# Two expert layers on one core: experts in groups of four with 32 places each, in place of pairs with 64

## The chip, the cores and the metric

One core of a Trainium2 chip runs the whole program once. The metric is the device time of that core in microseconds; lower is better. The program is a two-block network on 256 tokens of width 1024, in float32.

## The reference

The first block has two layers. Each is a mixer (a recurrence beside pooling in layer 0, attention beside a state-space model in layer 1) and then an expert layer. A second block of two layers follows. The change concerns the expert layers. Cut to what matters:

```python
def hier_moe(h, w_group, b_group, w_expert, b_expert, w_gate, w_up, w_down):
    '''Top-1 expert group, then top-2 experts in that group'''
    # 4 groups of 8 experts: each of 256 tokens goes to 2 of 32 experts
...
def routed_experts(hf, expert_idx, gates, w_gate, w_up, w_down):
...
    def run_block(args):
        tok, e, gt = args
        xb = h_pad[tok]
        hidden = jax.nn.silu(xb @ w_gate[e]) * (xb @ w_up[e])
        return (hidden @ w_down[e]) * gt[:, None].astype(xb.dtype)
```

`w_gate` and `w_up` of one expert are 1024 x 512, `w_down` is 512 x 1024, all float32: 6.29 MB an expert, 201.3 MB a layer. 512 places of tokens are spread over 32 experts, 16 on average. Evaluating the reference's routing on the given inputs, the fullest expert gets 26 tokens in layer 0 and 22 in layer 1.

## The kernel before

The order of the program is: recurrent mixer, expert layer 0, attention mixer, expert layer 1, second block. A scheduler orders each engine's instructions ahead of the run; on the chip each engine works through its list in order and waits on semaphores.

`moe` routes the tokens and then loops over 16 pairs of experts. `expert_pair` does, for a pair (64 places of an expert side by side make 128):

- **one-hot and gather** (L745, L757): VectorE makes a token-by-place matrix of zeros and ones. 32 products of 128 x 128 on TensorE pick the tokens out of the normed x (two float32r parts), giving `xe`, features on partitions, places along the free axis;
- **gate and up** (`both`, L763): for each of 8 blocks of features and each of the two experts one product with a stationary operand of 64 columns (that expert's places) and 512 moving columns of its weights. The two experts' results go to the two halves of the PSUM partitions. A float32 product is two MATMUL records;
- **hidden** (L784 to L790): silu on ScalarE, the product on VectorE, four transposes, a copy to SBUF (`hid`);
- **down** (L798): the same kind of products with `w_down`, by two halves of 512 output columns; ScalarE and VectorE scale by the gate and split in two parts (`y_hi` L801, `y_lo` L802);
- **scatter** (L808, L809, then L434): 8 products of 128 x 512 put the rows back to their tokens, VectorE adds to `x`.

`expert_weights` issues the loads of a pair on SyncE's queue (SP): 24 tiles of 512 KB (`wx`, 4 KB on each of 128 partitions), 8 of each matrix. A gate or up tile reads 4 KB in one piece for each partition, a down tile (`slab`, L734) two pieces of 2 KB. The tiles come by turns from three pools (`ring`, sizes `RINGS`): 17 tiles of the pool `u4`, 6 of the raw weights' pool `w`, 6 of the split weights' pool `hl`, 29 in all. In layer 0 from pair 4 on the ring is 6 + 6 + 6 = 18, because the next mixer's preparation (`middle`, that is `odd_prep` with `s5_prep`) takes `u4` tiles. A load waits until the products that read its place's last tile are done. The loads of the first pair are issued in `moe_ahead`, while the mixer still runs.

Before pair 4 stands a check, `overflowing`: each engine loads the largest count of an expert and branches. If it is over `SLOTS`, a loop over all experts follows for the tokens that found no place. With 64 places it is not taken on the given inputs.

The preparation of the attention mixer, a generator of small steps, runs between pairs 4 and 15 of layer 0, one or two steps a pair; its loads go through ScalarE's queue. In layer 1, `middle` is one small step.

Of the kernel before, what the change touches and what calls it, by code (L numbers as in the profile page):

```python
# [10 lines left out]
F32 = mybir.dt.float32  # L11
# [20 lines left out]
# where the odd mixer's projections and s5 steps stand in its attention  # L32
# [5 lines left out]
# where the even mixer's projections stand among its chunks  # L38
# [6 lines left out]
MAGIC = 1.5 * 2.0 ** 23  # added and taken off again, it rounds to an integer  # L45


def _parts(x):
    """x as a sum of three numbers of few bits"""
    out = []  # L50
    for bits in (10, 12, 24):
        e = math.floor(math.log2(abs(x)))
        step = 2.0 ** (e - bits + 1)
        v = math.floor(x / step) * step
        out.append(v)
        x -= v
    return out
# [29 lines left out]
class Stream:  # L87
    """Projections in the order in which they are added, by steps: the weights of a step are loaded
    and split ahead of its products."""
# [14 lines left out]
    def half(self):  # L104
        """half the products of a step"""
        self.products()
        self.then()
# [17 lines left out]
    def prepare(self):  # L125
        """the weights of the next steps"""
# [7 lines left out]
    def fetch(self, n=None):  # L134
        """the loads of all steps, or the first n, not their splits"""
# [3 lines left out]
    def through(self, n):  # L139
        """all steps of the first n items"""  # L140
# [4 lines left out]
class Model:  # L145
    def __init__(self, ctx, tc, I, out, taps=None):
# [13 lines left out]
        self.nsplit, self.on_pool = 0, 0     # of the weights' splits, every how many are gpsimd's  # L160
# [18 lines left out]
    def packed(self, name, parts):  # L179
        """a stage's constants, in one tile"""  # L180
# [12 lines left out]
    def u4(self, shape, dt=F32):  # L193
        """up to 4 KB a partition of longer-lived data"""
        return self.act.tile(list(shape), dt, tag="u4", name=self.name("u4"), bufs=23)

    def blocks(self, n, dt=F32):
        """n blocks [128, 256], as a list"""
# [51 lines left out]
    def rsqrt(self, out, src, scale, eps, shape):  # L250
        """out = (src * scale + eps) ** -0.5"""
# [25 lines left out]
    def split(self, hi, lo, src):  # L277
        """src (float32, SBUF) as hi + lo."""
# [16 lines left out]
    def proj_t(self, *a, **k):  # L295
        """ncol columns of h @ w, transposed: evac(block, psum [128, 256])."""
# [3 lines left out]
    def proj_t_steps(self, w, col0, xT, evac, ncol=512, pin=False):  # L300
        """proj_t, by its steps"""
# [15 lines left out]
    def item_t(self, w, col0, x, evac, ncol=512, pin=True, first=False):  # L317
        """proj_t for a stream; x() is the operand"""
# [24 lines left out]
    def item_n(self, w, col0, x, evac, row0=0, nk=None, pin=True):  # L343
        """512 columns of h @ w for a stream, tokens on partitions, over nk blocks of rows"""
# [21 lines left out]
    def proj_n(self, *a, **k):  # L366
        """ncol columns of h @ w, tokens on partitions: evac(token tile, psum [128, ncol])."""
# [32 lines left out]
    def rstd(self, t, eps=1e-6):  # L400
        """1 / rms of the rows of x's tile t, of which the mean squares are there"""
# [6 lines left out]
    def norm_t(self, gain, warm=0):  # L408
        """the normed x, transposed, as two float32r parts [128, 8, 256]."""
# [31 lines left out]
    def tick(self, first=1):  # L441
        """the next part of what x's new quarters, but the latest, give the router"""
# [7 lines left out]
    def out_proj(self, w, parts):  # L450
        """x += y @ w, y in parts: (first block of 128 features, hi, lo [128, 4, 256])"""
# [15 lines left out]
    def quarters(self, feeder):  # L467
        """x is there"""
# [6 lines left out]
    def begin(self):  # L475
        """before a stage's first step, if the one before leaves half of x's columns to be done between its steps"""
# [28 lines left out]
    def scales(self):  # L505
        """the tokens' scales: on partitions, and along the rows [128, 256]"""
# [8 lines left out]
    # -- mixture of experts -----------------------------------------------------  # L515
    def moe_ahead(self, l):
        """what an expert layer loads before its input is there"""
# [16 lines left out]
        return br, rings, self.expert_weights(l, 0, rings[0])  # L534
# [19 lines left out]
    def moe(self, l, ahead=None, middle=None, after=None):  # L554
# [10 lines left out]
        # normed x, tokens on partitions, as two parts (feature p * 8 + j at [j, p])  # L565
# [14 lines left out]
        def top(v, n):  # L580
            """the largest of [128, 2, n], and where it is first, as 0 and 1"""
# [18 lines left out]
        # by how many the experts of a group are outdone: those before count where equal  # L600
# [17 lines left out]
        # a token's place among those of an expert, from 1 on  # L618
# [8 lines left out]
        # the gates  # L627
# [42 lines left out]
        for pair in range(16):  # L670
            if pair == 4:
                self.keep_warm(WARM["check"])
                self.overflowing(l, over["n"], h_hi, h_lo, over["gates"])
            for _ in range((pair >= 4) + (pair in range(5, 12))):
                next(middle or iter(()), None)
            if pair == 15:
# [3 lines left out]
            if pair:  # L680
                weights = self.expert_weights(l, pair, rings[l == 0 and bool(middle) and pair >= 4], pair == 15 and after and after[1])
            self.rest = self.expert_pair(pair, weights, h_hi, h_lo, pos, gate, () if pair else (lambda: low(4), gates, beyond), pair == 15)
# [3 lines left out]
    def ring(self, *parts):  # L686
        """weight tiles of 4 KB, by turns out of the three pools"""
        tags = [t for t, m in enumerate(parts) for _ in range(m)]
        pools = ((self.act, "u4", 23), (self.wraw, "w", None), (self.wsp, "hl", None))
# [23 lines left out]
    def expert_weights(self, l, pair, tiles, between=None):  # L713
        """a pair of experts' weights"""
        nc, I = self.nc, self.I
        ee = (2 * pair, 2 * pair + 1)
# [1713 lines left out]
```

## Time and profile before

| what | value |
|---|---|
| median of 3 runs | 2854.08 us (2853.61 to 2862.12) |
| profiled execution, its span (the only time shown of it) | 2857.6 us |
| TensorE busy | 2676.7 us, 94% of the span |
| VectorE, ScalarE, GpSimd busy | 48%, 35%, 17% |
| loaded from HBM | 657.24 MB |
| expert layer 0, first gate product to last down product | 205.6 to 757.8 us |
| expert layer 1, the same | 950.9 to 1470.7 us |

A busy share of TensorE counts the time in which any product is under way. The profile gives, for each stretch, the share of full clock that was granted to TensorE (1.00 is 2.4 GHz) and the GB/s that the DMA engines moved. SPq rows are SyncE's issues of transfers; a row's second number is the time from the first to the last issue of the row.

### The profile page before, as it was taken

The page shows a single profiled execution, that of the slowest core. Times are in us where ns is not written, and L with a number is a line of the kernel's source. Part 1 is how long each engine was busy: PE and PEld are TensorE (multiplying, and loading weights), DVE is VectorE, ACT ScalarE, POOL GpSimd, SP SyncE. Part 2 cuts the span into 40 slices and gives each one's busy share as a digit, 9 for nine tenths or more (in the row PEclk, how much of TensorE's full clock was granted, in tenths as well). Part 3 has the DMA queues.
Part 4 walks back from the last instruction along what each step waited for, and adds up shares of the span by engine and source line. Part 5 has one row for each costly group of instructions (what it writes and reads, how often), then busy time and mean ns, then how long its engine had stood idle before and what let it go on. Part 6 is the DMA issues. An engine that isn't in the chain of part 4 may idle for free.

```text
span 2857.6 us, 43839 instructions
## 1 busy us (share of the span) xinstructions
PE 2676.7 (94%) x17593; PEld 2002.8 (70%) x17593; DVE 1359.5 (48%) x2263; ACT 1011.2 (35%) x1664; POOL 499.3 (17%) x428
## 2 busy tenths in 40 slices
PE   9989898889998999999999999999999999899998
PEld 8864344343577444443358998899988899899997
DVE  5641123231464321211146667746656576865664
ACT  6421121111235111111134546545444455554543
POOL 1110000010040000000022306511103132641110
PEclk9989899989999999999999999999999999999999
DMA  5359799989625889999945454355665555345564
GB/s 184 111 202 382 258 345 366 401 313 388 241 70 180 320 337 399 400 402 399 390 146 177 140 178 126 112 176 172 184 188 168 155 159 159 118 128 182 177 185 140
DMA packets 294463, 661.26 MB, mean 231 GB/s; under 512 B 36298, under 2 KB 42988, under 8 KB 294252
## 3 DMA queue, kind: packets, MB, share of 16 engines
q1 hardware_dynamic: 287796, 657.29, 66.5%
q8 instruction: 142, 2.33, 0.3%
q10 hardware_dynamic: 6456, 1.08, 0.3%
q14 instruction: 69, 0.57, 0.1%
HBM read 657.24 MB, written 1.05 MB: 230 GB/s over the span
## 4 chain that ended last, share of the span: by engine, by line
PE 50%; DVE 5%; POOL 3%; ACT 2%; issue 1%; DMA 1%; POOLq 0%; ACTq 0%; DVEq 0%; SPq 0%
PE ps_mm L291 36%; PE ps_mm L763 5%; PE ps_sml L798 3%; DVE whl L273 2%; PE ps_sml L757 1%; ACT whl L268 1%; DVE latri L2028 1%; POOL whl L273 1%; POOL xn L1979 1%; PE ps_sml L809 0%; PE ps_sml L1958 0%; POOL yf L1930 0%; DMA wx<-in_moe_w_gate_dram 0%; PE ps_sml L2078 0%; DMA wx<-in_moe_w_down_dram 0%
## 5 line engine op out<-in xcount | busy, mean ns | idle before, releaser
L291 PE MATMUL ps_mm<-u,whl 128*128 128x256 f32 x8448 | 1055.1, 286 | 27.5 <-POOL whl L273 17.4
L291 PEld LDWEIGHTS ps_mm<-u,whl 128*128 128x128 f32 x8448 | 1031.9, 193 | 40.8 <-POOL whl L273 19.4
L273 DVE TENSOR_TENSOR whl<-w,whl 128x1024 fp32r<-128x1024 f32 x432 | 557.7, 1295 | 418.4 <-ACT whl L268 411.6
L268 ACT ACTIVATE whl<-w 128x1024 fp32r<-128x1024 f32 x472 | 496.6, 1057 | 503.3 <-PE ps_mm L291 436.4
L763 PE MATMUL ps_mm<-wx,xe 128*64 128x512 f32 x2048 | 465.7, 607 | 0.0
L291 PE MATMUL ps_mm<-whl,u 128*128 128x512 f32 x1440 | 345.3, 396 | 6.1 <-ACT whl L268 3.2
L763 PEld LDWEIGHTS ps_mm<-wx,xe 128*64 128x64 f32 x2048 | 144.9, 139 | 266.5 <-issue 257.4
L291 PEld LDWEIGHTS ps_mm<-whl,u 128*128 128x128 f32 x1440 | 268.3, 189 | 66.6 <-DVE whl L273 4.1
L798 PE MATMUL ps_sml<-wx,hid 128*64 128x512 f32 x1024 | 253.3, 604 | 24.7 <-ACT hid L790 24.7
L798 PEld LDWEIGHTS ps_sml<-wx,hid 128*64 128x64 f32 x1024 | 74.4, 138 | 168.3 <-issue 130.3
L777 DVE CAST ohT<-ps_sml 128x256 fp32r<-128x256 f32 x32 | 13.6, 424 | 315.7 <-PE ps_sml L774 315.5
L802 DVE SCALAR_TENSOR_TENSOR y_lo<-ps_sml,sg,y_hi 128x512 fp32r<-128x512 f32 x64 | 48.0, 749 | 228.5 <-ACT y_hi L801 228.5
L405 POOL TENSOR_TENSOR rstd<-rstd,mhalf 128x1 f32<-128x1 f32 x18 | 11.9, 666 | 818.3 <-DVE rstd L404 809.1
L757 PEld LDWEIGHTS ps_sml<-oh,u 128*128 128x128 f32 x1024 | 136.8, 213 | 7.8 <-DVE oh L745 2.5
L273 POOL TENSOR_TENSOR whl<-w,whl 128x1024 fp32r<-128x1024 f32 x40 | 99.1, 2478 | 238.7 <-ACT whl L268 238.7
L757 PE MATMUL ps_sml<-oh,u 128*128 128x128 f32 x1024 | 136.9, 295 | 1.9 <-DVE oh L745 1.8
L801 ACT ACTIVATE y_hi<-ps_sml,sg 128x512 fp32r<-128x512 f32 x64 | 44.0, 688 | 258.8 <-PE ps_sml L798 258.8
L434 DVE TENSOR_TENSOR x<-x,ps_sml 128x512 f32<-128x512 f32 x128 | 83.6, 684 | 58.2 <-PE ps_sml L809 58.0
L790 ACT ACTIVATE hid<-ps_sml 128x512 f32<-128x512 f32 x32 | 19.1, 596 | 260.3 <-PE ps_sml L788 257.0
L785 DVE TENSOR_TENSOR sl<-sl,ps_mm 128x512 f32<-128x512 f32 x32 | 22.0, 688 | 170.3 <-PE ps_mm L763 145.6
L759 ACT ACTIVATE xe<-ps_sml 128x512 f32<-128x512 f32 x64 | 38.2, 597 | 180.7 <-PE ps_sml L757 180.7
L784 ACT ACTIVATE sl<-ps_mm 128x512 f32<-128x512 f32 x32 | 19.1, 597 | 208.4 <-PE ps_mm L763 192.1
(522 smaller groups left out, 2485.7 us busy)
## 6 DMA issues: line engine op xcount, KB each, us to landing
wx<-in_moe_w_down_dram SPq DMA_DIRECT2D x256, 512.0 KB
wx<-in_moe_w_gate_dram SPq DMA_DIRECT2D x256, 512.0 KB
wx<-in_moe_w_up_dram SPq DMA_DIRECT2D x256, 512.0 KB
w<-in_w_in_dram SPq DMA_DIRECT2D x208, 512.0 KB
w<-in_w_gate_up_dram SPq DMA_DIRECT2D x88, 512.0 KB
w<-in_w_down_dram SPq DMA_DIRECT2D x44, 512.0 KB
w<-in_ret_out_dram SPq DMA_DIRECT2D x32, 512.0 KB
w<-in_ssd_out_dram SPq DMA_DIRECT2D x32, 512.0 KB
```

What stands on the lines that cost most here:

```text
L268: ins = nc.scalar.activation(hi, raw, AF.Copy)
L273: eng.tensor_tensor(lo, raw, hi.bitcast(F32), op=OP.subtract)
L291: ins = nc.tensor.matmul(out, a, b, start=start and i == 0, stop=stop and i == 2)
L434: nc.vector.tensor_tensor(self.x[:, t, col0:col0 + ncol], self.x[:, t, col0:col0 + ncol], ps, op=OP.add)
L757: nc.tensor.matmul(pg[:, o:o + P], hh[t][:, j, :], oh2[:, t, :], start=j == j0 and i == 0, stop=j == j0 + 3 and i == 3)
L759: nc.scalar.activation(xe[:, j0:j0 + 4, :], pg.rearrange("p (a s) -> p a s", a=4), AF.Copy)
L763: nc.tensor.matmul(out[a * 64:(a + 1) * 64, :], xe[:, k, a * 64:(a + 1) * 64], w[k // 2][a][:, k % 2, :], start=k == 0, stop=k == NK - 1)
L798: nc.tensor.matmul(py[a * 64:(a + 1) * 64, :], hid[:, m, a * 64:(a + 1) * 64], wd[c][m // 2][a][:, m % 2, :], start=m == 0, stop=m == 3)
L801: nc.scalar.activation(y_hi[:, sc], py, AF.Copy, scale=sg)
L802: nc.vector.scalar_tensor_tensor(y_lo[:, sc], py, sg, y_hi[:, sc].bitcast(F32), op0=OP.mult, op1=OP.subtract)
L1979: G.tensor_tensor(f, hi, lo, op=OP.add)
L2028: eng.tensor_tensor(x_, tri.unsqueeze(1).to_broadcast([P, 4, P]), lar[part][:, c, h0:h0 + 4].bitcast(F32).unsqueeze(2).to_broadcast([P, 4, ...
```

## The change

- `SLOTS` goes from 64 to 32, and experts are taken by fours (`GROUP`): 8 groups in place of 16 pairs. A product of gate, up or down has a stationary operand of 32 columns and lands on its expert's quarter of the PSUM partitions, with its column position given. The number of these products stays, 512 MATMUL records for each of the three matrices and each layer. One-hot, gather, transposes, evacuations and scatter, which have 128 places at a time before and after, occur 8 times a layer, not 16.
- A group has 48 tiles. The down loads of all groups but the last take 128 whole rows of `w_down` (4 KB in one piece a partition). `down` then does both halves of the output columns at once, with the accumulators in the PSUM pool `mm`.
- The DMA scratch of the program is set to 1024 bytes, the pool `u4` goes from 23 to 26 tiles, the rings from 29 and 18 to 32 and 21.
- `moe_ahead` issues the gate loads and half of the up loads (24 tiles). The check stands before group 2, so after the same 8 experts. The `middle` steps come four at a time before groups 2 to 7. The gates of the places come from one VectorE operation with a mask (`own`), not two copies.

```diff
-SLOTS = 64
+SLOTS = 32
+GROUP = 4
-RINGS = (17, 6)
+U4 = 26
+RINGS = (20, 9)
+AHEAD = 6
...
-        for pair in range(16):
-            if pair == 4:
+        n_groups = 32 // GROUP
+        for g in range(n_groups):
+            last = g == n_groups - 1
+            if g == 2:
                 self.keep_warm(WARM["check"])
                 self.overflowing(l, over["n"], h_hi, h_lo, over["gates"])
-            for _ in range((pair >= 4) + (pair in range(5, 12))):
+            for _ in range(4 * (g >= 2)):
                 next(middle or iter(()), None)
...
+            for c in range(2 if last else 0):
+                if c and between:
+                    between()
+                for m in range(2):
+                    wd.append([load([P, 2, 512], slab(I["moe_w_down"][l, e], m * 2 * P, 2, c * 512, 512)) for e in ee])
+                    yield
+            for m in range(0 if last else 4):
+                wd.append([load([P, D], I["moe_w_down"][l, e][m * P:(m + 1) * P, :]) for e in ee])
+                yield
...
-        def both(out, w):
+        def every(out, w):
             for k in range(NK):
-                for a in range(2):
-                    nc.tensor.matmul(out[a * 64:(a + 1) * 64, :], xe[:, k, a * 64:(a + 1) * 64], w[k // 2][a][:, k % 2, :],
-                                     start=k == 0, stop=k == NK - 1)
+                for a, r in enumerate(rows):
+                    nc.tensor.matmul(out[r, :], xe[:, k, r], w[k // 2][a][:, k % 2, :], start=k == 0, stop=k == NK - 1,
+                                     tile_position=(0, a * SLOTS))
...
-        def down(c):
-            py = self.psum("sml")
+        def down(*cs):
+            pys = [self.psum("mm") for _ in cs]
             for m in range(4):
-                for a in range(2):
-                    nc.tensor.matmul(py[a * 64:(a + 1) * 64, :], hid[:, m, a * 64:(a + 1) * 64], wd[c][m // 2][a][:, m % 2, :],
-                                     start=m == 0, stop=m == 3)
+                for c, py in zip(cs, pys):
+                    for a, r in enumerate(rows):
+                        nc.tensor.matmul(py[r, :], hid[:, m, r], wd(c, m, a), start=m == 0, stop=m == 3, tile_position=(0, a * SLOTS))
...
-    nc = bacc.Bacc("TRN2", target_bir_lowering=False, num_devices=1)
+    nc = bacc.Bacc("TRN2", target_bir_lowering=False, num_devices=1, dynamic_dma_scratch_size=1024)
```

On TensorE, the gate products of the second pair begin like this before; `wx` are weight tiles, `xe` the gathered tokens, and 64x512 is the result.

```order
L763 MATMUL ps_mm_442_2398<-wx_414_2310,xe_439_2361 64x512
L763 MATMUL ps_mm_442_2398<-wx_415_2312,xe_439_2361 64x512
...
L763 MATMUL ps_mm_442_2398<-wx_416_2314,xe_439_2361 64x512
L763 MATMUL ps_mm_442_2398<-wx_417_2316,xe_439_2361 64x512
...
L763 MATMUL ps_mm_442_2398<-wx_418_2318,xe_439_2361 64x512
L763 MATMUL ps_mm_442_2398<-wx_419_2320,xe_439_2361 64x512
```

In the change the gate products of the first group begin like this, four experts' tiles by turns.

```order
L781 MATMUL ps_mm_415_2241<-wx_290_1802,xe_412_2204 32x512
L781 MATMUL ps_mm_415_2241<-wx_291_1804,xe_412_2204 32x512
L781 MATMUL ps_mm_415_2241<-wx_292_1806,xe_412_2204 32x512
L781 MATMUL ps_mm_415_2241<-wx_293_1808,xe_412_2204 32x512
...
L781 MATMUL ps_mm_415_2241<-wx_294_1810,xe_412_2204 32x512
L781 MATMUL ps_mm_415_2241<-wx_295_1812,xe_412_2204 32x512
```

Each tile serves two blocks of features, so that two tiles feed four products in a row before, and four tiles feed eight in the change.

On SyncE's queue, at the check in layer 0 before: the load of the count, then 12 loads of pair 4, of which the first and the last stand here, and then the branch.

```order
L697 TENSOR_LOAD cint_2228
L697 ISA x2
L720 DMA wx_3135<-in_moe_w_gate_dram 128x1024
L720 DMA wx_3137<-in_moe_w_gate_dram 128x1024
...
L734 DMA wx_3155<-in_moe_w_down_dram 128x2x512
L734 DMA wx_3157<-in_moe_w_down_dram 128x2x512
```

In the change at the same check:

```order
L705 TENSOR_LOAD cint_2292
L705 ISA x2
L731 DMA wx_3031<-in_moe_w_gate_dram 128x1024
L731 DMA wx_3033<-in_moe_w_gate_dram 128x1024
L731 DMA wx_3035<-in_moe_w_gate_dram 128x1024
L731 DMA wx_3037<-in_moe_w_gate_dram 128x1024
L731 DMA wx_3039<-in_moe_w_gate_dram 128x1024
L706 COMPARE_AND_BRANCH
```

Five loads stand between the count and the branch, not twelve; the other 43 of group 2 follow the branch.

## Rows read from the trace of the kernel before

**Rows 1.** The page: span, granted clock and GB/s in 40 slices.

```profile
span 2857.6 us, 43839 instructions
...
PEclk9989899989999999999999999999999999999999
...
GB/s 184 111 202 382 258 345 366 401 313 388 241 70 180 320 337 399 400 402 399 390 146 177 140 178 126 112 176 172 184 188 168 155 159 159 118 128 182 177 185 140
```

**Rows 2.** Timeline of TensorE, one pair: start us, us, line, operation, count.

```profile
1406.57 7.09 PE L763 MATMUL ps_mm<-wx,xe 128*64 128x512 f32 x32
...
1414.29 7.09 PE L763 MATMUL ps_mm<-wx,xe 128*64 128x512 f32 x32
...
1423.59 4.50 PE L798 MATMUL ps_sml<-wx,hid 128*64 128x512 f32 x18 [0.69 <-ACT hid L790]
...
1429.71 3.65 PE L798 MATMUL ps_sml<-wx,hid 128*64 128x512 f32 x14
...
1435.49 3.46 PE L757 MATMUL ps_sml<-oh,u 128*128 128x128 f32 x30
1438.88 7.09 PE L763 MATMUL ps_mm<-wx,xe 128*64 128x512 f32 x32
```

**Rows 3.** Windows: us, five engines' busy us, granted clock, DMA share, GB/s.

```profile
1184.00:1202.00 18.00, 16.43 (x77) 5.63 (x73) 2.32 (x7) 1.88 (x3) 0.00 (x0) 1.00 1.03 409
1206.00:1212.00 6.00, 5.22 (x36) 4.16 (x34) 2.04 (x3) 1.28 (x2) 0.00 (x0) 1.00 1.05 387
195.00:210.00 15.00, 13.27 (x50) 9.42 (x52) 5.63 (x29) 2.89 (x5) 0.00 (x0) 0.57 0.01 1
1066.00:1072.00 6.00, 5.76 (x25) 2.56 (x22) 3.41 (x6) 0.69 (x1) 0.00 (x0) 1.00 0.42 126
388.00:400.00 12.00, 10.47 (x54) 3.83 (x52) 3.76 (x14) 1.41 (x3) 0.00 (x0) 1.00 0.82 254
424.00:436.00 12.00, 5.01 (x24) 1.73 (x20) 3.36 (x8) 0.21 (x1) 0.00 (x0) 0.86 0.94 244
575.00:600.00 25.00, 19.30 (x69) 11.01 (x70) 12.04 (x36) 1.88 (x3) 5.64 (x12) 0.66 0.52 196
1072.00:1337.00 265.00, 243.47 (x1174) 108.28 (x1172) 45.69 (x95) 30.04 (x48) 0.00 (x0) 0.98 1.03 400
225.00:250.00 25.00, 24.14 (x126) 11.37 (x128) 5.11 (x11) 3.73 (x6) 0.00 (x0) 1.00 0.96 357
```

**Rows 4.** Timeline of TensorE's weight loads in the first gate products.

```profile
212.04 0.14 PEld L763 LDWEIGHTS ps_mm<-wx,xe 128*64 128x64 f32 x2 [0.29 <-issue]
212.47 0.14 PEld L763 LDWEIGHTS ps_mm<-wx,xe 128*64 128x64 f32 x2 [0.29 <-issue]
```

**Rows 5.** Timeline of TensorE in the attention mixer: products with 32 stationary columns.

```profile
783.50 0.38 PE L1734 MATMUL ps_mm<-s_ad,u 128*32 128x128 f32 x2
783.72 0.38 PE L1736 MATMUL ps_mm<-s_ad,u 128*32 128x127 f32 x2
```

**Rows 6.** Timeline of SyncE's queue: first issues after the ring was full, and the check.

```profile
209.74 2.39 SPq L720 DMA_DIRECT2D wx<-in_moe_w_up_dram  x2
...
955.01 8.26 SPq L720 DMA_DIRECT2D wx<-in_moe_w_up_dram  x8
...
321.05 0.38 SPq L734 DMA_DIRECT2D wx<-in_moe_w_down_dram  x1
329.87 1.30 SPq L720 DMA_DIRECT2D wx<-in_moe_w_gate_dram  x3
```

**Rows 7.** Waits of SyncE's queue over the span: total us, times, longest.

```profile
SPq L720 <- PE ps_mm L763: 191.2, 92, 20.5
...
SPq L734 <- DMA s_bre<-in_s_b_re_dram: 9.2, 1, 9.2
```

**Rows 8.** Timeline of TensorE: first gate products of layers, last down products.

```profile
205.61 9.61 PE L763 MATMUL ps_mm<-wx,xe 128*64 128x512 f32 x32
...
755.83 1.93 PE L798 MATMUL ps_sml<-wx,hid 128*64 128x512 f32 x6
...
950.88 9.02 PE L763 MATMUL ps_mm<-wx,xe 128*64 128x512 f32 x32
...
1468.72 1.93 PE L798 MATMUL ps_sml<-wx,hid 128*64 128x512 f32 x6
```

More of the change, by code (lines that the diff above doesn't have):

```diff
@@ L533, in moe_ahead @@
         self.feeder = self.feed
-        return br, rings, self.expert_weights(l, 0, rings[0])
+        weights = self.expert_weights(l, 0, rings[0])
+        for _ in range(AHEAD):
+            next(weights[0])
+        return br, rings, weights
     def feed(self, t, half):
@@ L679, in moe @@
                 self.feeder = after and after[0]
-            if pair:
-                weights = self.expert_weights(l, pair, rings[l == 0 and bool(middle) and pair >= 4], pair == 15 and after and after[1])
-            self.rest = self.expert_pair(pair, weights, h_hi, h_lo, pos, gate, () if pair else (lambda: low(4), gates, beyond), pair == 15)
+            if g:
+                weights = self.expert_weights(l, g, rings[l == 0 and bool(middle) and g >= 2], last, last and after and after[1])
+            self.rest = self.expert_group(g, weights, h_hi, h_lo, pos, gate, () if g else (lambda: low(4), gates, beyond), last)
         if not after:
@@ L711, in overflowing, with expert_weights @@
                 self.overflow(l, e, hT, gov)
-    def expert_weights(self, l, pair, tiles, between=None):
+    def expert_weights(self, l, g, tiles, last=False, between=None):
         nc, I = self.nc, self.I
-        ee = (2 * pair, 2 * pair + 1)
-        def part(name, e, i):
-            w = next(tiles)([P, 2, 512])
-            nc.sync.dma_start(w, I[name][l, e].rearrange("(p j) f -> p j f", j=NK)[:, i * 2:(i + 1) * 2, :])
-            return w
-        wg = [[part("moe_w_gate", e, i) for e in ee] for i in range(4)]
-        wu = [[part("moe_w_up", e, i) for e in ee] for i in range(4)]
-        wd = []
-        for c in range(2):
-            if c and between:
-                between()
-            wd.append([])
-            for m in range(2):
-                wd[-1].append([])
-                for e in ee:
-                    w = next(tiles)([P, 2, 512])
-                    nc.sync.dma_start(w, slab(I["moe_w_down"][l, e], m * 2 * P, 2, c * 512, 512))
-                    wd[-1][-1].append(w)
-        return wg, wu, wd
@@ L738, in expert_pair, with load, loads @@
-    def expert_pair(self, pair, weights, h_hi, h_lo, pos, gate, meanwhile, last):
-        nc = self.nc
-        wg, wu, wd = weights
-        oh = self.s("oh", [P, 2, 2, SLOTS], F32R)
+        ee = range(GROUP * g, GROUP * g + GROUP)
+        wg, wu, wd = [], [], []
+        def load(shape, src):
+            w = next(tiles)(shape)
+            nc.sync.dma_start(w, src)
+            return w
+        def loads():
+            for to, name in ((wg, "moe_w_gate"), (wu, "moe_w_up")):
+                for i in range(4):
+                    to.append([load([P, 2, 512], I[name][l, e].rearrange("(p j) f -> p j f", j=NK)[:, i * 2:(i + 1) * 2, :]) for e in ee])
+                    yield
[7 more added lines that the diff above has]
+                wd.append([load([P, D], I["moe_w_down"][l, e][m * P:(m + 1) * P, :]) for e in ee])
+                yield
@@ new lines, in expert_weights, with expert_group @@
+        down = (lambda c, m, a: wd[2 * c + m // 2][a][:, m % 2, :]) if last else (lambda c, m, a: wd[m][a][:, c * 512:(c + 1) * 512])
+        return loads(), wg, wu, down
+    def expert_group(self, g, weights, h_hi, h_lo, pos, gate, meanwhile, last):
+        nc = self.nc
+        loads, wg, wu, wd = weights
+        for _ in loads:
+            pass
+        mine = slice(GROUP * g, GROUP * g + GROUP)
+        rows = [slice(a * SLOTS, (a + 1) * SLOTS) for a in range(GROUP)]
+        oh = self.s("oh", [P, 2, GROUP, SLOTS], F32R)
@@ L773, in expert_pair @@
         for t in range(2):
-            nc.tensor.matmul(po[:, T:T + 2], oh2[:, t, :].bitcast(F32), gate[:, t, 2 * pair:2 * pair + 2],
+            nc.tensor.matmul(po[:, T:T + GROUP], oh2[:, t, :].bitcast(F32), gate[:, t, mine],
                              start=t == 0, stop=t == 1)
@@ L777, in expert_pair @@
         nc.vector.tensor_copy(ohT, po[:, :T])
-        sg = self.s("sg", [P, 1])
-        nc.vector.tensor_copy(sg[0:64], po[0:64, T:T + 1])
-        nc.vector.tensor_copy(sg[64:128], po[64:128, T + 1:T + 2])
+        sg, sj = self.s("sg", [P, 1]), self.s("sj", [P, GROUP])
+        nc.vector.scalar_tensor_tensor(sj, po[:, T:T + GROUP], 1.0, self.own, op0=OP.mult, op1=OP.mult, accum_out=sg)
         pu = self.psum("mm")
-        both(pu, wu)
+        every(pu, wu)
         sl = self.s("sl", [P, 512])
@@ L816, in end @@
             yield -1
-        down(0)
         if last:
+            down(0)
             scatter(0)
@@ L821, in expert_pair @@
             return end(self.feeder)
-        down(1)
+        down(0, 1)
         scatter(0)
@@ L2298, in shared @@
         self.ones = self.const("ones", [P, P])
[L2299 removed]
+        t = self.const("places", [P, SLOTS + 4 + 64 + GROUP])
         self.iota, self.falling = t[:, :SLOTS], t[:, SLOTS:SLOTS + 4]
[L2301 removed]
+        self.earlier = t[:, SLOTS + 4:SLOTS + 68].rearrange("p (i j) -> p i j", i=8)
+        self.own = t[:, SLOTS + 68:]
 @with_exitstack
```

22 lines of the change are left out of this document (11 added, 11 removed).

## The prediction

> **What bounds the kernel now.** I read the page's slices first [rows 1]. The reader is to see that TensorE keeps a granted clock of 0.9 to 1.0 nearly everywhere, and that the slices of layer 1 hold some 400 GB/s, while those of layer 0 go up and down between 258 and 401. So the two expert layers sit near two limits at once, and the question is which one ends last.
>
> TensorE's timeline of one pair comes next [rows 2]: gate 7.09 us, up 7.09, down 4.50 + 3.65 = 8.15, gather 3.46; the next pair's gate begins 1438.88 - 1406.57 = 32.31 us later. Products take 22.33 us, and the other 9.98 (gather, transposes, scatter, small waits) belong to 128 places, not to a number of experts. Against that stand the transfers [rows 3]: 409 GB/s while 4 KB pieces arrive (1184 to 1202) and 387 while the 2 KB pieces of the down tiles do (1206 to 1212), so 0.5243 MB take 1.28 us and 1.355 us, and a pair's 24 tiles 16 x 1.28 + 8 x 1.355 = 31.3 us. TensorE's 32.3 us end last, by one microsecond. The waits of SyncE's queue say so too [rows 7]: 191.2 us in 92 waits, for gate and up products that still read a place of the ring. The window 1072 to 1337 shows both full: TensorE busy 243 of 265 us, 400 GB/s [rows 3].
>
> The layers' ends are in [rows 8]: layer 0 from 205.61 to 755.83 + 1.93 = 757.8, layer 1 from 950.88 to 1468.72 + 1.93 = 1470.7, that is 552 and 520 us.
>
> **What the change does to TensorE.** Two products with 64 columns start together, and the next two 0.43 us later [rows 4]. If four products with 32 columns do the same, a matrix of a group takes the 16 steps of 0.43 us that a matrix of a pair takes now, a group costs what a pair costs, about 32.3 us, and TensorE needs 8 x 32.3 = 259 us a layer, not 520. No row shows four at once. The nearest are products with 32 columns in the attention mixer, which follow each other: two records of 128 columns take 783.72 - 783.50 = 0.22 us [rows 5], so 0.11 each, or 0.43 for 512. Bounds for a group: all four at once, 22.3 + 10.0 = 32.3 us; two at once as today, 44.7 + 10.0 = 54.7; one after another, 192 records x 0.43 + 10.0 = 92.6. I take 32.3, because rows 4 show halves of the columns running side by side and the new positions are quarters of the same kind.
>
> **What it does to the transfers.** The bytes stay. A group has 48 tiles, 48 x 1.28 = 61.4 us, more than 32.3 and more than 54.7: the transfers become the bound, and between "four at once" and "two at once" the time hardly differs. The ring holds 32 of the 384 tiles of a layer before the first gate product; today the DMA engines then stand still (1 GB/s from 195 to 210, [rows 3]). The other 352 follow: 336 in pieces of 4 KB, 176.2 MB / 409 = 430.7 us, and 16 down tiles of the last group in pieces of 2 KB, 16 x 1.355 = 21.7, together 452.4. Two 512 KB tiles of the next stage stand in the same queue, 2.6. The whole rows alone save (128 - 16) x 0.075 = 8.4 us a layer, contained in these numbers. A larger ring costs nothing here; in layer 0 it falls to 21 tiles, 27 us of transfers, so TensorE may be late by that much before the queue stands still.
>
> The start is SyncE's first issue after the full ring: 209.74 and 955.01 [rows 6], 4.1 us after the first gate product. To the first bytes I add 1.5, chosen between 0 and those 4.1.
>
> **Layer 0.** 209.7 + 1.5 + 452.4 + 2.6 = 666.2. To this come:
> - *The check.* The queue stands from 321.05 to 329.87 [rows 6]. In the same place in layer 1 the six microseconds from 1066 moved 126 GB/s in place of about 405 [rows 3]: (1 - 126/405) x 6 = 4.1 lost. It stays, with five loads ahead of the branch, not twelve.
> - *The small loads of the next mixer.* SyncE waited 9.2 us for one of them [rows 7], and around two of them 254 and 244 GB/s moved (388 to 400, 424 to 436, [rows 3]): (1 - 254/405) x 12 + (1 - 244/405) x 12 = 9.3. Today they hide in part behind TensorE; a bound of transfers pays them whole. 0 to 9.3, I take 9.3.
> - *Late products.* VectorE and TensorE work in order, and preparation stands between the experts' operations. From 575 to 600 that held TensorE at a clock of 0.66, with 196 GB/s [rows 3]: (1 - 196/405) x 25 = 12.9 lost. Now 29 us of slack a group stand behind a ring of 27 us, but four steps come together. Nothing to two such stalls, 26; I take 8.
> - *The tail.* After the last tile its products, evacuation and whatever clock was lost in the waits, 0 to 5 us (a gate at a clock of 0.57 took 9.61 us against 7.09, [rows 3, 8]); I take 5.
>
> 666.2 + 4.1 + 9.3 + 8 + 5 = 692.6, against 757.8: **65 us less.**
>
> **Layer 1.** 955.0 + 1.5 + 452.4 + 2.6 + 4.1 + 5 = 1420.6, against 1470.7: **50 us less.** There is almost no preparation there.
>
> The two mask copies that go and the one operation that comes are work of VectorE, at 48% of the span, and hidden; the mixers and the second block keep their order, and I give them no change. So the span goes from 2857.6 to 2857.6 - 65 - 50 = 2742.6. That profiled execution was 3.5 us over the median of the runs; on the median's scale I predict **2739**.
>
> **A rule against it.** The one long window of full transfers shows 400 GB/s over 265 us, and pieces of 4 KB 409 [rows 3]. The Trainium skill, "DMA: Bandwidth & Descriptors", section "Where 436 GB/s comes from", says that transfers from HBM to SBUF are bound by the HBM side, about 358 GB/s for a core. By it the 352 tiles would take an estimated 515 us, as long as a layer takes now, and the change would bring nothing; the trace of this core, which runs alone, disagrees with 400.
>
> **Rivals.**
> 1. *The four columns don't run together* (slower). For it speaks that every product with 32 columns in the trace follows the one before it [rows 5]; against it, that halves do run together [rows 4] and that those in the mixer have no neighbour in another quarter. One at a time gives 8 x 92.6 = 741 us a layer, 189 and 221 more than now: about 3260. It decides when a group takes over 2 x 32.3 = 64.6 us, so when fewer than 82.6 / 54.6 = 1.5 run at once on average. 2%. The Trainium skill, "TensorEngine Tiling (Array Packing)", section "Performance Considerations", gives a fourfold tiling for 32 columns; no run shown so far bears that out.
> 2. *The transfers don't hold 409 GB/s.* At the 357 of the window 225 to 250 [rows 3] the 352 tiles take 184.5 MB / 357 = 517 us, 65 us more a layer than I count, and the time is about 2869, no gain. Against it: that window stands between a ring just filled and TensorE at 24.1 of 25 us, so TensorE slowed the transfers. 3%.
> 3. *The clock falls in the waits.* TensorE will wait half of each group, and where it waited the granted clock was 0.57 and 0.66 [rows 3]. If all ran at 1.2 GHz, a group would take 2 x 32.3 = 64.6 us, and the layers 517 each: 38 us less than now, about 2816. For it: the first gate products take 9.61 and 9.02 us [rows 8]. Against it: a TensorE that is busy gets 1.00 again in the next windows, so the loss limits itself. 6%.
> 4. *The preparation starves the ring in layer 0*, at every group from 2 to 5: two stalls more than I took, 26 + 8 = 34 in place of 8, and about 2765; it lies within my case's own range.
>
> The full branch behind the check is no rival: 26 and 22 tokens at most need no more than 32 places.
>
> **How the numbers follow.** The forecast with its sizes has 88%, rivals 1 to 3 have 11, an unnamed other 1. Low: no late products (-8), no tails (-10), half of the small loads (-5), the checks hidden (-8): 2708, say 2705. High: rival 4 (+26) and half of the way to rival 3 (a quarter of its 77, +20, with the checks at twice their price): about 2790. This holds some 85 of the 88, and leaves the rivals out. About 0.3% is what a measurement of this kernel can tell from no change; faster by more than that: the forecast and rival 3 and the unnamed, 0.95; within it: rival 2 in part, 0.02; slower: rival 1 and the rest of rival 2, 0.03.
>
> **What the changed profile would show.** Right: slices at 400 GB/s through both layers with dips only at the check and in layer 0's preparation; weight loads of 32 columns four to each 0.43 us; SyncE's long waits no more for products; TensorE idle about half of each group, waiting for weight tiles, at a lower clock; the last down product of layer 0 near 693, and layer 1 some 470 us long. Wrong: four weight loads in 0.86 or 1.7 us (rival 1), a flat 350 GB/s (rival 2), gate groups of 14 us (rival 3), holes in the transfers in each group from 2 to 5 (rival 4). The sum fails if a group's tiles arrive in other than 61 us while nothing holds SyncE.

## The result, and the profile after

The changed kernel's median is 2744.72 us (2743.51 to 2745.94, 4 runs), that of before, run beside it, 2855.48: a ratio of 0.961, 95% interval 0.9597 to 0.9624. The forecast was 2739. The profiled execution has a span of 2742.0 us; the forecast's sum for the span was 2742.6.

From the page of the changed kernel: the span, the busy row of TensorE, its granted clock and the GB/s in 40 slices, which answer to [rows 1].

```profile
span 2742.0 us, 41790 instructions
...
PE 2555.1 (93%) x16793; PEld 1839.6 (67%) x16793; DVE 1260.2 (46%) x2071; ACT 950.0 (35%) x1567; POOL 497.9 (18%) x428
...
PEclk9989989999998999999999999999999999999999
...
GB/s 190 117 213 369 344 406 409 409 409 375 111 81 272 408 379 409 409 409 409 340 177 124 177 139 123 146 178 179 185 188 171 132 174 142 116 142 178 180 192 131
```

Both expert layers now have slices at 409 GB/s, where before they went up and down from 258 to 402. TensorE's busy share has hardly moved, from 94 to 93%: whoever reads only that row would take TensorE for the bound still.

The ends of the two layers, from TensorE's timeline of the changed kernel (start us, us, line, operation, count):

```profile
201.10 8.75 PE L781 MATMUL ps_mm<-wx,xe 128*32 128x512 f32 x64
210.93 7.07 PE L781 MATMUL ps_mm<-wx,xe 128*32 128x512 f32 x64
...
684.36 1.92 PE L816 MATMUL ps_mm<-wx,hid 128*32 128x512 f32 x14
...
883.14 15.92 PE L781 MATMUL ps_mm<-wx,xe 128*32 128x512 f32 x128
...
1352.72 1.90 PE L816 MATMUL ps_mm<-wx,hid 128*32 128x512 f32 x10
```

Layer 0 runs from 201.10 to 686.28, 485.2 us where it took 552.2 [rows 8]; layer 1 from 883.14 to 1354.62, 471.5 for 519.8. That is 67.0 and 48.3 us less, with 65 and 50 forecast. The rest nearly cancels: layer 0 starts 4.5 us earlier, the stretch between the layers is 3.7 longer, what follows 0.4 longer. -4.5 - 67.0 + 3.7 - 48.3 + 0.4 = -115.7; the spans differ by 115.6. Why layer 0 starts earlier no run tells.

The second row also settles the first step of the forecast: with all tiles there, the 64 records of the first up matrix take 7.07 us, what 32 took before (7.09, [rows 2]). Its weight loads, from the timeline of TensorE's loads, answer to [rows 4]:

```profile
212.24 0.13 PEld L781 LDWEIGHTS ps_mm<-wx,xe 128*32 128x32 f32 x4 [0.30 <-issue]
212.67 0.13 PEld L781 LDWEIGHTS ps_mm<-wx,xe 128*32 128x32 f32 x4 [0.30 <-issue]
```

Four start together every 0.43 us. The Trainium skill, "TensorEngine Tiling (Array Packing)", section "Performance Considerations", gives a fourfold tiling for 32 columns, and here the trace agrees.

What a group looks like when transfers bound it, from TensorE's timeline in layer 1 (in brackets the idle time before and what ended it); it answers to [rows 2]:

```profile
1041.04 3.79 PE L774 MATMUL ps_sml<-oh,u 128*128 128x128 f32 x32
...
1065.33 1.05 PE L781 MATMUL ps_mm<-wx,xe 128*32 128x512 f32 x2 [0.24 <-DMA wx<-in_moe_w_up_dram]
1066.61 1.04 PE L781 MATMUL ps_mm<-wx,xe 128*32 128x512 f32 x2 [0.23 <-DMA wx<-in_moe_w_up_dram]
1067.89 2.31 PE L781 MATMUL ps_mm<-wx,xe 128*32 128x512 f32 x12 [0.23 <-DMA wx<-in_moe_w_up_dram]
1070.45 1.04 PE L781 MATMUL ps_mm<-wx,xe 128*32 128x512 f32 x2 [0.24 <-DMA wx<-in_moe_w_up_dram]
...
1103.00 1.22 PE L774 MATMUL ps_sml<-oh,u 128*128 128x128 f32 x9
```

A tile arrives every 1.28 us (1065.33, 1066.61, 1067.89). Mostly the two records that can go then run on one quarter of the columns, for 1.04 us, and TensorE waits 0.23 us for the next tile; every third such row, with 12 records, catches up on what was left. From gather to gather it is 1103.00 - 1041.04 = 61.96 us, with 61.4 forecast for 48 tiles. The waits of SyncE's queue over the span say the same. Before, those for products of gate and up were 191.2 us at the loads of gate and up [rows 7] and 68.1 us more at the loads of down:

```profile
SPq L731 <- DMA wx<-in_moe_w_gate_dram: 212.3, 215, 4.7
...
SPq L731 <- DMA wx<-in_moe_w_down_dram: 198.8, 217, 3.5
SPq L731 <- DMA wx<-in_moe_w_up_dram: 194.8, 215, 1.9
...
SPq L731 <- PE ps_mm L781: 51.2, 19, 19.9
```

The queue now waits for its own earlier transfers. Of the 51.2 us left, the waits for the first gate products with a full ring take 20 a layer.

Where transfers were lost, from the windows of the changed kernel (us, five engines' busy us, granted clock, DMA share, GB/s), which answer to [rows 3]:

```profile
205.00:231.00 26.00, 24.24 (x198) 8.39 (x190) 4.33 (x14) 2.57 (x4) 0.00 (x0) 1.00 0.99 385
231.00:260.00 29.00, 23.99 (x121) 8.02 (x120) 4.90 (x26) 4.56 (x6) 0.00 (x0) 0.94 0.87 327
285.00:310.00 25.00, 20.78 (x78) 9.57 (x77) 9.01 (x44) 5.50 (x11) 0.00 (x0) 0.94 0.88 335
310.00:335.00 25.00, 20.68 (x100) 6.04 (x99) 2.10 (x8) 2.48 (x3) 0.00 (x0) 0.86 0.96 307
384.00:400.00 16.00, 16.00 (x96) 8.90 (x96) 0.15 (x1) 1.19 (x2) 0.07 (x2) 0.64 1.02 404
440.00:660.00 220.00, 196.93 (x864) 57.47 (x856) 35.45 (x96) 12.66 (x22) 11.57 (x24) 1.00 1.03 408
960.00:985.00 25.00, 22.98 (x93) 10.34 (x91) 4.15 (x7) 2.57 (x4) 0.00 (x0) 1.00 0.87 327
1041.04:1226.16 185.12, 167.99 (x727) 50.94 (x727) 16.73 (x37) 11.29 (x18) 0.00 (x0) 1.00 1.03 409
1325.00:1354.60 29.60, 24.53 (x105) 7.22 (x104) 6.19 (x10) 5.89 (x12) 0.72 (x1) 0.94 0.98 339
```

Against 409 GB/s the first four lose 26 x (1 - 385/409) = 1.5, 5.8, 4.5 and 6.2 us: the start, small loads of the next mixer's constants, the check, and small loads of its tables. From 440 to 660 nothing is lost. In layer 1 the check loses 25 x (1 - 327/409) = 5.0, and the layer's end, from 1325 on, 29.6 x (1 - 339/409) = 5.1. The 185 us from 1041 on show TensorE busy for 168 of them at a granted clock of 1.00, while 409 GB/s arrive.

### The profile page after: what moved, and what is told of

Its sections match the earlier page's. It is cut to its first block, busy times and chain, and to the rows that moved or that the text cites. A ratio compares the mean times of both kernels' runs of the same rounds, so it can differ in the third digit from the quotient of the medians.

```text
span 2742.0 us, 41790 instructions
## 1 busy us (share of the span) xinstructions
PE 2555.1 (93%) x16793; PEld 1839.6 (67%) x16793; DVE 1260.2 (46%) x2071; ACT 950.0 (35%) x1567; POOL 497.9 (18%) x428
## 4 chain that ended last, share of the span: by engine, by line
PE 42%; DMA 13%; DVE 4%; POOL 3%; ACT 2%; issue 1%; SPq 0%; POOLq 0%; ACTq 0%; DVEq 0%
PE ps_mm L294 37%; DMA wx<-in_moe_w_up_dram 4%; DMA wx<-in_moe_w_gate_dram 4%; DMA wx<-in_moe_w_down_dram 4%; DVE whl L276 2%; ACT whl L271 1%; POOL whl L276 1%; DVE latri L2046 1%; PE ps_sml L1976 1%; POOL yf L1948 1%; PE ps_sml L2096 1%; POOL xn L1997 0%; PE ps_mm L816 0%; PE ps_sml L2060 0%; DVE cv L1912 0%
## 5 line engine op out<-in xcount | busy, mean ns | idle before, releaser
L781 PE MATMUL ps_mm<-wx,xe 128*32 128x512 f32 x2048 | 444.8, 617 | 61.2 <-DMA wx<-in_moe_w_up_dram 41.1
L781 PEld LDWEIGHTS ps_mm<-wx,xe 128*32 128x32 f32 x2048 | 87.4, 111 | 390.1 <-DMA wx<-in_moe_w_up_dram 198.1
L816 PE MATMUL ps_mm<-wx,hid 128*32 128x512 f32 x1024 | 269.9, 600 | 14.1 <-ACT hid L807 11.0
L816 PEld LDWEIGHTS ps_mm<-wx,hid 128*32 128x32 f32 x1024 | 71.9, 109 | 194.7 <-issue 121.6
L820 DVE SCALAR_TENSOR_TENSOR y_lo<-ps_mm,sg,y_hi 128x512 fp32r<-128x512 f32 x32 | 24.0, 751 | 264.0 <-ACT y_hi L819 262.6
L819 ACT ACTIVATE y_hi<-ps_mm,sg 128x512 fp32r<-128x512 f32 x32 | 22.0, 687 | 240.9 <-PE ps_mm L816 240.6
L2241 POOL TENSOR_TENSOR yT<-yT,rb 128x256 f32<-128x256 f32 x44 | 40.9, 948 | 203.7 <-ACT yT L2240 203.7
L774 PE MATMUL ps_sml<-oh,u 128*128 128x128 f32 x512 | 72.2, 306 | 5.1 <-issue 3.4
L774 PEld LDWEIGHTS ps_sml<-oh,u 128*128 128x128 f32 x512 | 69.5, 221 | 11.1 <-DVE x L437 5.2
L1912 DVE SCALAR_TENSOR_TENSOR cv<-ps_mm,cols_cw,cv 128x253 f32<-128x253 f32 (+1 forms) x144 | 64.3, 476 | 25.9 <-ACT cv L1909 25.2
```

The costliest lines, as they stand in the source:

```text
L774: nc.tensor.matmul(pg[:, o:o + P], hh[t][:, j, :], oh2[:, t, :], start=j == j0 and i == 0, stop=j == j0 + 3 and i == 3)
L781: nc.tensor.matmul(out[r, :], xe[:, k, r], w[k // 2][a][:, k % 2, :], start=k == 0, stop=k == NK - 1, tile_position=(0, a * SLOTS))
L816: nc.tensor.matmul(py[r, :], hid[:, m, r], wd(c, m, a), start=m == 0, stop=m == 3, tile_position=(0, a * SLOTS))
L1912: V.scalar_tensor_tensor(acc[:, s:], ps[:, :T - s], cw[i][:, b + m:b + m + 1], acc[:, s:], op0=OP.mult, op1=OP.add)
L2241: nc.gpsimd.tensor_tensor(sil[s0][:, m, :], sil[s0][:, m, :], sc[1], op=OP.mult)
```

## The experiments

Each is an edit of the changed kernel. A ratio is to the kernel before, timed beside it; the change's own is 0.961, and 0.9615 (0.9598 to 0.9632) in a second series, median 2748.73, run with this expectation: 

> The change as it is, once more, for comparison on one chip: 0.961 of the time before, about 2745.

**Two experts at a time.** Products, and loads in the same order, by halves of a group; of the edit, the loop of gate and up:

```diff
-            for k in range(NK):
-                for a, r in enumerate(rows):
+            for k, a in ((k, a) for b in range(0, GROUP, 2) for k in range(NK) for a in range(b, b + 2)):
+                for r in rows[a:a + 1]:
```

> Products of a group by two experts and then the other two, loads in the same order: only two columns' quarters can run at once. My theory (transfers bound): a group then needs 44.7 + 10.0 = 54.7 us on TensorE, still under the 61.4 us of its 48 tiles, so the time stays within 10 us of 2744.7. Rival (TensorE still bounds, as its busy share of 93% suggests): each of 16 groups grows by 22.3 us, +357, about 3102.

2753.12 us, ratio 0.9634 (0.9614 to 0.9654), 0.2% over the change. Where all tiles were there, an up matrix took this, from TensorE's timeline:

```profile
405.26 12.25 PE L786 MATMUL ps_mm<-wx,xe 128*32 128x512 f32 x64
```

12.25 us for 7.07, and yet layer 0 took 488.9 us (200.57 to 689.5) and layer 1 469.9 (886.66 to 1356.5), against 485.2 and 471.5. Work on TensorE that grew by 5 us a matrix cost the layers nothing to speak of: the rival, 3102, is out. The run also tells how much of the change the bound needed. Three such matrices and the 10.0 us of work on 128 places make an estimated 3 x 12.25 + 10.0 = 46.8 us a group, under the 61.4 of the transfers, and the pairs of before ran two at a time as well. So doing the gather, the transposes and the scatter once for four experts and not twice is already enough to bring TensorE under the transfers; four quarters at once give room that the time does not use.

**One expert at a time.** The same edit with one in place of two.

> One expert after another in gate, up and down: one quarter of the columns at a time. My theory: 192 records x 0.43 + 10.0 = 92.6 us a group, over the 61.4 us of transfers, so TensorE bounds: 741 us a layer in place of 485 and 471.5, about 3270. Rival (the four never ran at once, the products were issued one after another all the time): no change, 2745.

3041.97 us (one run). TensorE bounds again, but with 75.4 us a group, not 92.6. Its timeline in layer 1, and its weight loads at the passage from one expert to the next:

```profile
1421.71 3.79 PE L779 MATMUL ps_sml<-oh,u 128*128 128x128 f32 x32
...
1472.02 22.59 PE L821 MATMUL ps_mm<-wx,hid 128*32 128x512 f32 x64 [0.69 <-ACT hid L812]
...
1497.14 3.12 PE L779 MATMUL ps_sml<-oh,u 128*128 128x128 f32 x26
```

```profile
1430.18 0.11 PEld L786 LDWEIGHTS ps_mm<-wx,xe 128*32 128x32 f32 x1 [0.32 <-issue]
1430.61 0.14 PEld L786 LDWEIGHTS ps_mm<-wx,xe 128*32 128x32 f32 x3 [0.32 <-issue]
1431.04 0.14 PEld L786 LDWEIGHTS ps_mm<-wx,xe 128*32 128x32 f32 x2 [0.29 <-issue]
1431.47 0.14 PEld L786 LDWEIGHTS ps_mm<-wx,xe 128*32 128x32 f32 x2 [0.29 <-issue]
1431.93 0.11 PEld L786 LDWEIGHTS ps_mm<-wx,xe 128*32 128x32 f32 x1 [0.32 <-issue]
```

Within an expert one load in 0.43 us, as expected. At a passage seven loads start in three such steps: the next expert's first products start beside the last ones of the expert before, and 64 records take 22.59 us, not 27.5. So quarters of the columns have to run together for the transfers to bound, but two at a time are enough.

**Everything but the fours.** `SLOTS` 64, `GROUP` 2, the check before group 4, the preparation's steps as before; whole rows for down, the larger rings and the mask stay:

```diff
-SLOTS = 32
-GROUP = 4
+SLOTS = 64
+GROUP = 2
```

> All parts of the change except the fours: pairs with 64 places, with whole rows for down, the larger rings and the mask. My theory: TensorE bounds again at 30.4 to 32.3 us a pair; 2830 to 2855. Rival (rings and whole rows brought most of it): 24 tiles of 1.28 us make 30.7 us a pair, 16 of them 491 us a layer, less the prefetched 41 us: about 2745 to 2760.

2814.72 us, ratio 0.9845 (0.9827 to 0.9863), 1.55% less than before, out of the range of both. Layer 0 took 520.7 us, layer 1 504.9. From TensorE's timeline of this kernel:

```profile
1254.86 7.14 PE L816 MATMUL ps_mm<-wx,hid 128*64 128x512 f32 x32 [0.69 <-ACT hid L807]
1262.76 1.32 PE L826 MATMUL ps_sml<-y_hi,ohT 128*128 128x512 f32 x4 [0.76 <-ACT y_hi L819]
1263.92 1.10 PE L827 MATMUL ps_sml<-y_lo,ohT 128*128 128x512 f32 x4
```

Down stands in one piece of 7.14 us, with nothing of the first half's scatter between. Before it stood in two [rows 2]. A pair takes 31.0 us, not 32.3, and the layers' later pairs follow at that pace. There both limits stand together: in four of these pairs (1203.1 to 1327.1) TensorE waits for no tile, and 409 GB/s arrive, by which 24 tiles take 30.7 us.

**The same with pieces of 2 KB for down.** To tell whole rows from the order of products, the edit above with this one:

```diff
-                wd.append([load([P, D], I["moe_w_down"][l, e][m * P:(m + 1) * P, :]) for e in ee])
+                wd.append([load([P, 2, 512], slab(I["moe_w_down"][l, e], m // 2 * 2 * P, 2, m % 2 * 512, 512)) for e in ee])
```

> As the pairs with all other parts of the change, but the down tiles in two pieces of 2 KB again; both halves of down's products still stand together. My theory (it is the order of the products on TensorE, 31.0 us a pair without the first half's scatter between, not the whole rows, that made the pairs 45 us faster): the transfers' 31.3 us a pair bound now, 0.3 us x 32 pairs = 10 us over the pairs, about 2820 to 2825. Rival (whole rows did it): back near the time before, 2850.

2843.78 us, ratio 0.9931 (0.991 to 0.9952), nearer to the rival. Its timeline of TensorE shows why:

```profile
1237.28 6.22 PE L816 MATMUL ps_mm<-wx,hid 128*64 128x512 f32 x26 [0.69 <-ACT hid L807]
1243.46 0.51 PE L826 MATMUL ps_sml<-y_hi,ohT 128*128 128x512 f32 x1
...
1245.14 1.93 PE L816 MATMUL ps_mm<-wx,hid 128*64 128x512 f32 x6
```

The code asks for both halves together, but the program's scheduler split them again, and a pair takes 32.3 us, as in the kernel before. So with pairs the whole rows do bring some 25 us. The run brings back the pieces of 2 KB and the split products at once, and so it does not part them by itself. But the transfers with pieces of 2 KB take 31.3 us a pair, less than 32.3: they did not bound, and of the 1.3 us a pair at least 1.0 belongs, by this sum, to the order in which the scheduler sets TensorE's products. What remains between this kernel and the one before, some 20 us, lies nearly all in layer 0 (533.3 for 552.2); whether the larger ring or the shorter preparation stalls bring it was not told apart.

**Pieces of 2 KB in the change.** The same line edited with groups of four.

> The down tiles of all groups in two pieces of 2 KB a partition, the products as in the change. My theory (transfers bound, pieces of 2 KB at 387 GB/s): 112 tiles a layer x 0.075 us x 2 layers = 17 us more, about 2761. Rival (whole rows matter only for the order of the products on TensorE, which stays here): no change, 2745.

2761.73 us, ratio 0.9663 (0.9639 to 0.9686), 0.5% over the change: 13 us over its second series, 17 over its first, with 17 expected. Here, where transfers bound, the rows' form has the price of the transfers.

**The ring of before.** The DMA scratch of before comes back with it; of the edit, the sizes:

```diff
-U4 = 26
-RINGS = (20, 9)
+U4 = 23
+RINGS = (17, 6)
```

> The ring of before (29 tiles, 18 in layer 0 from group 2 on, 23 tiles in the pool, the scratch as before). My theory: three tiles fewer are there when the layer starts, 3 x 1.28 x 2 layers = 8 us more, and up to 8 us more where layer 0's slack behind 18 tiles is too short: 2752 to 2760. Rival (the ring's size is without effect once transfers bound): 2745.

2759.87 us, ratio 0.9635 (0.9605 to 0.9665); the runs spread widely (2743.45 to 2766.45), and the interval doesn't part it from the change. The profiled execution is the longest of them. Its layers took 496.7 and 476.0 us, 11.5 and 4.5 more: the second is near the price of three tiles (3.8), the first would be that and less slack behind 18. It fits, on one profile, and is not shown by the times.

**Without the check.**

```diff
-                self.overflowing(l, over["n"], h_hi, h_lo, over["gates"])
+                pass
```

> Without the check and its branch (it leaves out the loop for tokens that find no place, which these inputs don't need). My theory: the hole in the transfers at the check, some 4 us a layer, goes: 8 us less, about 2736. Rival (the hole belongs to the small loads beside it, or the ring fills it up again): no change, 2745.

2742.28 us, ratio 0.959 (0.9565 to 0.9615), not parted from the change by its interval. The layers of the profile are 482.2 and 466.5 us, 3.0 and 5.0 less. Its span shows none of that beside the first profile of the change (2742.4 and 2742.0), because what follows the layers took 6.5 us longer, and 8.5 us beside that of the second series (2750.9): profiles of one program differ by as much as this run was to find. The window of layer 1's check is filled:

```profile
960.00:985.00 25.00, 24.92 (x122) 10.85 (x119) 3.96 (x7) 2.57 (x4) 0.00 (x0) 1.00 1.03 409
```

**Products in one go.** The blocks of features from last to first, so that TensorE has nothing to do until the last four of a matrix' 16 tiles come:

```diff
-            for k in range(NK):
+            for k in reversed(range(NK)):
...
-            for m in range(4):
+            for m in reversed(range(4)):
```

> Within each matrix the blocks of features from the last to the first, so that TensorE waits for the last of a matrix' 16 tiles and then does all its products in one go. My theory of the clock (TensorE kept its full clock in the change because its products came one tile at a time): longer waits, and a granted clock well under 1.00 in the expert layers, matrices of 7 to 14 us. Layer 1 with 32 places then loses under 5 us, since 3 x 14 + 10 = 52 us is under 61.4; layer 0 with 21 places stops the queue while 16 wait: 5 to 13 us a group, 30 to 80 in all. Rival (the clock stays at 1.00 whatever the order, and only the places matter): the same times, with the clock at 1.00.

2797.86 us (one run). In layer 1, TensorE's timeline, its weight loads at the start of the first of these matrices, and windows of two groups and of two pieces of that matrix:

```profile
1223.35 10.80 PE L781 MATMUL ps_mm<-wx,xe 128*32 128x512 f32 x64 [3.14 <-DMA wx<-in_moe_w_gate_dram]
1243.72 10.90 PE L781 MATMUL ps_mm<-wx,xe 128*32 128x512 f32 x64 [9.57 <-DMA wx<-in_moe_w_up_dram]
```

```profile
1225.82 0.18 PEld L781 LDWEIGHTS ps_mm<-wx,xe 128*32 128x32 f32 x2 [1.10 <-DMA wx<-in_moe_w_gate_dram]
1227.10 0.16 PEld L781 LDWEIGHTS ps_mm<-wx,xe 128*32 128x32 f32 x8 [1.10 <-DMA wx<-in_moe_w_gate_dram]
1227.56 0.13 PEld L781 LDWEIGHTS ps_mm<-wx,xe 128*32 128x32 f32 x4 [0.30 <-issue]
```

```profile
1153.40:1215.87 62.47, 39.65 (x244) 17.78 (x243) 5.48 (x13) 3.77 (x6) 0.00 (x0) 0.81 1.03 409
1215.87:1277.37 61.50, 39.66 (x244) 15.50 (x243) 5.56 (x13) 3.77 (x6) 0.00 (x0) 0.81 1.03 409
...
1223.35:1225.00 1.65, 1.65 (x3) 0.33 (x4) 0.00 (x0) 0.00 (x0) 0.00 (x0) 0.50 1.01 405
1227.00:1229.00 2.00, 2.00 (x21) 0.68 (x24) 0.00 (x0) 0.00 (x0) 0.00 (x0) 1.00 0.99 391
```

Now TensorE is busy 40 of 61.5 us and its mean granted clock is 0.81, but layer 1's groups take 61.5 and 62.5 us, as in the change. The layer took 479.3 us, 8 more than in the change, where under 5 were expected.

A matrix takes 10.8 us for 7.07, and this is not the clock's doing. Its first loads start when the first of the last four tiles is there, and for each of the other three the loads wait 1.10 us. From the last one's arrival at 1227.10 on, four start every 0.43 us, at a granted clock of 1.00. The clock is at 0.50, that is 1.2 GHz, at the matrix' start, when the next tile is not there anyway. So the lower clock of rival 3 of the prediction was real as a behaviour, and by these rows it cost next to nothing in layer 1.

Layer 0, where the ring has 21 places, took 520.9, 36 more. SyncE's queue waits there 128.5 us for products of the three matrices, 30.3 in the change. By this it is the places held back that cost, but no run holds the products back at the full clock.

**Preparation spread out.** Two steps before each of groups 0 and 1, three before each later one, run in two series:

```diff
-            for _ in range(4 * (g >= 2)):
+            for _ in range(3 * (g >= 2) + 2 * (g < 2)):
```

> Steps of the next mixer's preparation: two before each of groups 0 and 1, three before each later one, in place of four before groups 2 to 7. My theory: the preparation's holes in the transfers cost 15 to 20 us of layer 0, and what falls into the time when the ring is full is free: 5 to 10 us less, 2735 to 2740. Rival (steps ahead of group 0 delay its gather and the start of the transfers): 5 us more, 2750.

> The spread steps once more, beside the change on one chip. My theory: of the holes in layer 0's transfers (5.8 us at the odd constants, 4.5 at the check, 6.2 at the tables' small loads) spreading took about 8, so 0.3% under the change: 2737. Rival (the difference to the change was one between chips): the same as the change.

2741.29 us, ratio 0.9582 (0.9565 to 0.96), and, on one chip with the change, 2741.85, ratio 0.9591 (0.9574 to 0.9607) against 0.9615 (0.9598 to 0.9632): some 0.25% faster both times, with intervals that overlap a little. Layer 0 of the second took 476.1 us, 485.9 in the change beside it, but began 2.2 us later. Its windows, which answer to those of the change above:

```profile
231.00:260.00 29.00, 24.07 (x126) 8.94 (x126) 5.64 (x13) 2.65 (x5) 0.00 (x0) 1.00 1.06 354
285.00:310.00 25.00, 19.93 (x67) 7.35 (x64) 9.32 (x15) 1.38 (x2) 1.05 (x2) 0.94 0.85 330
310.00:335.00 25.00, 22.31 (x136) 12.21 (x139) 6.23 (x18) 1.78 (x3) 1.05 (x2) 0.65 1.03 410
```

The hole from 310 to 335 is gone, the one from 231 smaller, the check's stays. Its two ratios are as low as that of the kernel without the check, and neither is clearly parted from the change.

**The first step still earlier.** Before the layer's norm, the rest as spread out:

```diff
+        for _ in range(l == 0):
+            next(middle or iter(()), None)
         self.drain()
```

> The first preparation step before the expert layer's norm, when the queue is far from its limit, then two steps before groups 0 and 1 and three before each later one. My theory: the small loads of the constants leave the layer's transfers whole and those of the tables come into the time when the ring is full: 10 to 14 us under the change, 2731 to 2735. Rival (the steps stand ahead of the norm and the router on ScalarE and VectorE, on the path that sets the first gate product): layer 0 starts 3 to 10 us later and nothing is won, 2745.

2746.88 us, ratio 0.9616 (0.96 to 0.9633): nothing was won, as the rival had it. Layer 0 is 480.3 us long, 5.6 less than in the change beside it, but begins at 206.65, 5.4 us later. This fits the rival's reason, the steps on the path to the first gate product; the path itself was not traced.

## Why the prediction was right

**The bound moved to the transfers, as worked out.** Four columns' quarters run together (7.07 us a matrix), and the layer is first issue plus 352 tiles plus holes. Layer 0: from the first issue after the full ring, 204.71, to 686.28 are 481.6 us, of which 455.0 are the 452.4 for the tiles and 2.6 for two of the next stage; 26.6 remain, 27.9 were forecast. Layer 1: 886.80 to 1354.62, 467.8 us, 12.8 over the 455.0, 10.6 forecast. The kernel with two experts at a time shows that TensorE had room, the one with a single expert that it bounds again when that room is gone. The rule that speaks against it, the 358 GB/s for a core's side of HBM of the Trainium skill, "DMA: Bandwidth & Descriptors", section "Where 436 GB/s comes from", does not hold here: 409 over 185 us, on a core that runs alone.

**Its parts came out less evenly than the sum.** Of layer 0's terms the check took 4.5 us (4.1 forecast); the small loads 5.8 + 6.2 = 12.0 (9.3), for the constants' loads had not been counted, which before stood at 307 to 314, where 230 GB/s moved; the late products nothing (8): from 384 to 400 TensorE is late, its clock at 0.64, but 404 GB/s go on, since the ring's slack held. With 1.5 at the start, 8.6 remain for the tail (5); what they consist of no window tells. In layer 1 the check took 5.0 (4.1) and the end 5.1 (5). There SyncE's queue stands, by its timeline, between these two issues:

```profile
1326.62 1.87 SPq L267 DMA_DIRECT2D w<-in_w_in_dram  x2
1337.10 5.23 SPq L731 DMA_DIRECT2D wx<-in_moe_w_down_dram  x8
```

The second half's down tiles wait until the products of the first half's let go of their places, at 1336.5. That wait was not in the sum; the tail's 5 us, meant for products and clock, have its size by luck. Luck is also that the span came out within 0.6 us of the sum: the terms' errors cancel, layer 0's start was not forecast to move, and the second series' profile of the same kernel is 9 us longer.

**What failed.** "TensorE idle about half of each group, waiting for weight tiles, at a lower clock" was wrong. Its work is half, but it is spread over the arrival of the tiles, mostly on one quarter of the columns at a time: busy 168 of 185 us, clock 1.00. Rival 3 thus had no ground in this order of products; with the products held back the mean clock falls to 0.81, and even then a group in layer 1 does not take the 64.6 us that the rival gave it. And 0.43 us a record with one expert at a time overstated that bound, 92.6 for 75.4 us a group. The range's high end contradicts itself: half of the way to rival 3 would be 38 of its 77 us, and the sum takes a quarter.

**What was right for a narrower reason.** The text gave joint down and whole rows a price in transfers alone. With pairs they take 1.3 us a pair off TensorE and, with the rings and the mask, 45 us off the time, two fifths of the 111 us of the change. The forecast did not suffer, because a bound by transfers doesn't ask where TensorE's room comes from; had the sum been made from TensorE's savings, it would have.

## What to carry to other kernels

Once a change makes another resource the bound, compute the new time from that resource alone (first issue, bytes at the rate of the nearest row, holes) and not from what the old one saves. Busy share is no test for it: work that waits piece by piece for its operands looks busy; the queue's waits and the flat GB/s say more, and an experiment that slows the suspected engine decides, since both limits can stand together, as in the kernel with pairs. What could hide behind the old bound, small loads above all, is paid in full then, so look for every hole in the transfers, not only for those at which the old bound stood still.

## What was not expected of the hardware

Products on different quarters of the columns overlap not only when they alternate: with one expert after another, seven weight loads start in the three steps of 0.43 us at a passage, and 64 records take 22.59 us, not 27.5. TensorE kept a granted clock of 1.00 over 185 us through waits of 0.23 us after most tiles, with half of its work gone. With the products held back, and waits of 3 and 9.6 us ahead of a matrix, the mean was 0.81. But in the matrix shown the clock was at 0.50 as the work began and at 1.00 once the last tile was there, so that the mean says little about what the lower clock costs.
